# A two-layer diffusion trunk on one core: modulation products 512 columns wide, loaded from GpSimd's queue, and the state-space table products issued in whole runs

## The chip, the cores and the metric

The kernel runs on one core of one Trainium2 chip. The metric is the device time of one execution in microseconds (us). The time before is the median of three runs, 1136.7 us (1134.99 to 1141.31). The engines are named as the profile names them: PE (TensorE matmul), PEld (its weight loads), DVE (VectorE), ACT (ScalarE), POOL (GpSimd) and SP (SyncE, which only issues transfers here).

## The reference: what is computed

Two layers, in float32, on 128 context tokens and 256 latent tokens of width 1024. Only what bears on the change stands here:

```python
def ada_mods(cvec, p):
    m = jax.nn.silu(cvec) @ p['ada_w'] + p['ada_b']      # (1024) @ (1024 x 6144)
    return jnp.split(m[:, None, :], 6, axis=-1)          # shift, scale, gate, twice

def trunk_layer(x, cvec, p, mixer_fn):
    sh1, sc1, g1, sh2, sc2, g2 = ada_mods(cvec, p)
    mixed, extra = mixer_fn(rmsnorm(x, p['norm1_g']) * (1 + sc1) + sh1)
    x = x + g1 * mixed
    x = x + g2 * conv_ffn(rmsnorm(x, p['norm2_g']) * (1 + sc2) + sh2, p)
    return x, extra
```

The mixer has four parallel parts: neighbourhood attention, a bidirectional complex-diagonal state-space scan (S5), grouped-query attention and latent attention. The kernel does the scan in chunks of 8 tokens. For that it makes chunk tables from the S5 parameters alone, for each layer and each block of four channel groups: `SE` (inputs to chunk states), `SF` (states to outputs) and `SK` (the products inside a chunk). They are written to DRAM and loaded again in the scan.

## The kernel before, in words

**The main work.** All large products are `mm3` (L299 to L302): three float32r matmuls per 128 x 128 weight block, with weights and activations each split into a high and a low part. 1440 such triples make 4320 matmuls of 128 x 128 x up to 386 columns. Weight pieces of 512 KB come over SP's queue into three buffers with the tag `raw` (`piece`, L278), and ACT and DVE split them (`split1`).

**Modulation.** The vectors `silu(c) @ ada_w` for both token kinds are made a third of a layer at a time by `ada_steps(l, g)` (L317). The first third of layer 0 is made elsewhere (`first`), so five thirds are left. For each of the eight 128-row blocks `kc`, the weights come as two pieces `h` of 128 x 1024 in buffers of their own (tag `ada`, three buffers, `NADA`). The stationary operand is `cw[:, kc]`, 128 x 32 (two useful columns). Four matmuls per piece write 256 columns each to four different 32-partition strips of one PSUM bank `pa`: 16 pieces and 64 matmuls per third, 80 pieces and 320 matmuls in all. A piece is one step of the generator. Steps stand as the letter `A` in the string `SPEC`, which sets the order in which the mixer's streams advance; more are taken in the feed-forward part. The results are needed late, so these steps fill gaps between other work.

**Tables.** `s5_tables(l, ...)` (L693) runs over four blocks `b`. DVE makes `eb` and `ca` by complex multiplication (`cmul`), PE transposes eight 128 x 128 blocks of `eb` (L712), and PE makes the products `kd` (L728): 16 matmuls of 64 rows, 32 output partitions and 128 columns, over directions `d` (upper or lower 64 rows, two PSUM buffers), real and imaginary part `i` (accumulated) and group `g` (the 32-partition strip). Layer 0's tables are made beside the first mixer's projections. Layer 1's are made in layer 0's feed-forward part, at a lowered priority (L1334 to L1341).

**What sets the order.** The framework's scheduler orders each engine's instructions by priority and by when it takes operands to be ready. Each engine then runs its own list strictly in order, and waits on semaphores. The same holds for a queue of transfers: SP and POOL each issue in the order of their list, and a transfer into a reused buffer waits there for the buffer's readers. The helper `adjacent(calls)` (L247) issues the last call first and lets the others follow directly, so that the list holds them side by side. It is already used for the sums of squares and for the two heads in step.

**What else uses POOL's queue.** Stores of `SE`, `SF`, `SK` (L714, L721, L738), their loads in the scan (L749, L823), outputs, small clears, and one addition of the mask to the attention bias per pair of heads (L1168), which waits for the bias to be loaded over SP.

Of the kernel before, what the change touches and what calls it, by code (L numbers as in the profile page):

```python
# [20 lines left out]
L = 2  # L21
# [107 lines left out]
def _prepare(a):  # L129
    f = np.float32  # L130
    a = {n: np.asarray(v) for n, v in a.items()}
# [5 lines left out]
    def col(v, p=128):  # L137
# [7 lines left out]
    r["ada"] = np.stack([w.reshape(8, 128, 4, 2, 256).transpose(0, 3, 1, 2, 4)  # L145
                         for l in range(L) for w in np.split(a["ada_w"][l], 3, axis=1)][1:]
                        ).reshape(5, 8, 2, 128, 1024)
# [69 lines left out]
def _program(tc, I, O):  # L217
# [60 lines left out]
    def piece(src, n, tag="raw", eng=SY):  # L278
        raw = wp.tile([128, 1024], F32, name="raw", tag=tag, bufs=NRAW if tag == "raw" else NADA)
        eng.dma_start(raw[:, :n], src)  # L280
        return raw
# [35 lines left out]
    def ada_steps(l, g):  # L317
        acc = pa()
        for kc in range(8):
            for h in range(2):  # L320
                raw = piece(I["ada"][3 * l + g - 1, kc, h], 1024, "ada")
                for c in range(4):
                    PE.matmul(acc[32 * c:32 * c + 32, 256 * h:256 * h + 256], cw[:, kc],  # L323
                              raw[:, 256 * c:256 * c + 256], start=kc == 0 and h == 0,
                              stop=kc == 7 and h == 1)
                if kc < 7 or h == 0:
                    yield
        ar = kp.tile([128, 512], F32, name="ar", tag="sqz", bufs=3)
# [363 lines left out]
    def s5_tables(l, qp, cmp, bc, dd):  # L692
# [8 lines left out]
        for b in range(4):  # L701
# [6 lines left out]
            for i in range(2):  # L708
                e = kp.tile([128, 512], F32, name="tbo", tag="sqz", bufs=3)
                tr = pt()  # L710
                for g in range(4):
                    PE.transpose(tr[:, 128 * g:128 * g + 128], eb[:, i, g].rearrange("p j c -> p (j c)"), ident)  # L712
                A.activation(e, tr, AF.Copy)
                G.dma_start(SE[l][:, b, 512 * i:512 * i + 512], e)  # L714
# [9 lines left out]
            for d in range(2):  # L724
                h = slice(64 * d, 64 * d + 64)
                for i in range(2):
                    for g in range(4):
                        PE.matmul(kd[d][32 * g:32 * g + 32, 0:128], bb[i][h, 4 * b + g],  # L728
                                  ca[h, i, g, 2 * d:2 * d + 8].rearrange("p t c -> p (t c)"), start=i == 0,
                                  stop=i == 1)  # L730
# [865 lines left out]
```

## Time and profile before

| | us |
|---|---|
| median of the three runs | 1136.7 |
| the profiled execution, its own time | 1145.2 |
| its span, first to last instruction | 1143.2 |
| PE busy / DVE busy / ACT busy / POOL busy | 1074.7 / 798.3 / 581.0 / 86.8 |
| mean granted TensorE clock | 0.97 |

In a row of the timeline, the first number is the start in us from the span's start, the second the time from the first start to the last end; `x16` counts records. A float32 matmul leaves two records on PE, a float32r matmul and a transposition one. Matmuls are pipelined, so that what one costs is read from the start of one to the start of the next. In the lists of waits and the costliest groups, the engine's idle time stands with what ended it. The page's own span is 2 us shorter than the time of that execution.

### The profile page before, as it was taken

How to read it: one execution, taken by the hardware profiler on the slowest of the kernel's cores; microseconds unless marked ns; L12 is line 12 of the kernel's file. 1: busy time of each engine (PE TensorE's matmuls, PEld its weight loads, DVE VectorE, ACT ScalarE, POOL GpSimd, SP SyncE). 2: the span in 40 equal slices, each digit the busy share in tenths (PEclk: the TensorE clock that was granted, in tenths of full speed). 3: DMA queues.
4: the chain of work that ended last, by engine and by line, in shares of the span. 5: the costliest groups of instructions: out<-in, count | busy, mean ns of one | idle time of the engine just before them, and what ended most of it. 6: DMA issues, size and time to landing. Idle time of an engine off the chain costs nothing.

```text
span 1143.2 us, 18675 instructions
## 1 busy us (share of the span) xinstructions
PE 1074.7 (94%) x6724; PEld 911.6 (80%) x6724; DVE 798.3 (70%) x1934; ACT 581.0 (51%) x1251; POOL 86.8 (8%) x197
## 2 busy tenths in 40 slices
PE   6899889979999999999999989899799999999998
PEld 3677475437979999996999877545498999999998
DVE  6888478836979964676976886557468875467653
ACT  3654436426676543454456735563468554345532
POOL 4113111000100000000110220000000000000000
PEclk8899889979999999999999999999899999999999
DMA  9988847453465434443455664436133433443343
GB/s 342 298 274 270 264 128 270 139 178 129 147 196 161 138 100 138 147 117 113 136 153 159 180 222 159 111 124 230 39 111 99 135 113 114 137 138 117 117 133 100
DMA packets 64699, 182.18 MB, mean 159 GB/s; under 512 B 15840, under 2 KB 19168, under 8 KB 64608
## 3 DMA queue, kind: packets, MB, share of 16 engines
q1 hardware_dynamic: 55456, 152.52, 42.5%
q0 software_dynamic: 8576, 28.16, 7.8%
q8 instruction: 53, 0.87, 0.3%
q10 hardware_dynamic: 576, 0.32, 0.1%
q14 instruction: 38, 0.31, 0.1%
HBM read 166.19 MB, written 14.78 MB: 158 GB/s over the span
## 4 chain that ended last, share of the span: by engine, by line
PE 77%; DVE 9%; DMA 7%; ACT 4%; issue 1%; POOL 1%; SPq 0%; ACTq 0%; DVEq 0%; POOLq 0%
PE pz L300 12%; PE pz L301 11%; PE pz L302 11%; PE psc L300 8%; PE psc L301 8%; PE psc L302 8%; DMA raw<-ada 5%; PE pa L323 3%; PE psc L958 2%; PE ptr L971 2%; DVE lo L293 1%; PE po L996 1%; PE ptr L728 1%; DMA bias<-rpb 1%; PE psc L783 1%
## 5 line engine op out<-in xcount | busy, mean ns | idle before, releaser
L292 ACT ACTIVATE hi<-raw 128x512 fp32r<-128x512 f32 (+2 forms) x396 | 228.5, 585 | 285.6 <-PE pz L301 111.8
L293 DVE TENSOR_TENSOR lo<-raw,hi 128x512 fp32r<-128x512 f32 (+2 forms) x396 | 252.8, 640 | 158.5 <-ACT hi L292 114.4
L300 PE MATMUL pz<-ah,hi 128*128 128x386 f32 (+1 forms) x616 | 216.3, 353 | 3.7 <-ACT ah L430 2.2
L301 PE MATMUL pz<-al,hi 128*128 128x386 f32 (+1 forms) x616 | 213.7, 347 | 0.9 <-DVE al L431 0.8
L302 PE MATMUL pz<-ah,lo 128*128 128x386 f32 (+1 forms) x616 | 212.8, 346 | 0.0
L300 PEld LDWEIGHTS pz<-ah,hi 128*128 128x128 f32 x616 | 117.3, 191 | 23.5 <-issue 17.6
L301 PEld LDWEIGHTS pz<-al,hi 128*128 128x128 f32 x616 | 118.1, 192 | 7.0 <-issue 3.4
L302 PEld LDWEIGHTS pz<-ah,lo 128*128 128x128 f32 x616 | 117.9, 191 | 5.0 <-issue 4.4
L300 PE MATMUL psc<-ah,hi 128*128 128x386 f32 (+1 forms) x336 | 115.5, 344 | 0.3 <-DVE zr L461 0.3
L301 PE MATMUL psc<-al,hi 128*128 128x386 f32 (+1 forms) x336 | 115.4, 343 | 0.0
L302 PE MATMUL psc<-ah,lo 128*128 128x386 f32 (+1 forms) x336 | 115.0, 342 | 0.0
L323 PE MATMUL pa<-raw,cw 128*32 128x256 f32 x640 | 61.1, 418 | 18.7 <-DMA raw<-ada 18.6
L300 PEld LDWEIGHTS psc<-ah,hi 128*128 128x128 f32 x336 | 64.2, 191 | 1.6 <-issue 0.8
L301 PEld LDWEIGHTS psc<-al,hi 128*128 128x128 f32 x336 | 64.4, 192 | 0.4 <-issue 0.4
L302 PEld LDWEIGHTS psc<-ah,lo 128*128 128x128 f32 x336 | 64.3, 191 | 0.3 <-issue 0.2
L300 PE MATMUL pz<-fh,hi 128*128 128x384 f32 x176 | 59.7, 340 | 0.0
L300 PE MATMUL psc<-fh,hi 128*128 128x384 f32 x176 | 59.5, 338 | 0.0
L302 PE MATMUL psc<-fh,lo 128*128 128x384 f32 x176 | 59.5, 338 | 0.0
L302 PE MATMUL pz<-fh,lo 128*128 128x384 f32 x176 | 59.4, 337 | 0.0
L301 PE MATMUL psc<-fl,hi 128*128 128x384 f32 x176 | 59.1, 336 | 0.0
L301 PE MATMUL pz<-fl,hi 128*128 128x384 f32 x176 | 59.0, 336 | 0.0
L323 PEld LDWEIGHTS pa<-raw,cw 128*32 128x32 f32 x640 | 18.6, 114 | 45.2 <-DMA raw<-ada 25.5
(425 smaller groups left out, 1948.2 us busy)
## 6 DMA issues: line engine op xcount, KB each, us to landing
raw<-wup SPq DMA_DIRECT2D x88, 512.0 KB, 3.6
raw<-ada SPq DMA_DIRECT2D x80, 512.0 KB, 5.0
raw<-win SPq DMA_DIRECT2D x30, 512.0 KB, 5.1
raw<-wdn SPq DMA_DIRECT2D x32, 384.0 KB, 3.1
raw<-wdn SPq DMA_DIRECT2D x32, 320.0 KB, 2.9
a<-ada SPq DMA_DIRECT2D x16, 512.0 KB, 5.8
raw<-wout SPq DMA_DIRECT2D x16, 512.0 KB, 3.7
se<-tbo POOLq DMA_DIRECT2D x16, 256.0 KB, 4.2
```

The costliest lines, as they stand in the source:

```text
L292: A.activation(hi[:, :n], raw[:, a:b], AF.Copy)
L293: V.tensor_tensor(lo[:, :n], raw[:, a:b], hi[:, :n].bitcast(F32), op=OP.subtract)
L300: PE.matmul(out, wh, xh, start=start, stop=False)
L301: PE.matmul(out, wh, xl, start=False, stop=False)
L302: PE.matmul(out, wl, xh, start=False, stop=stop)
L323: PE.matmul(acc[32 * c:32 * c + 32, 256 * h:256 * h + 256], cw[:, kc], raw[:, 256 * c:256 * c + 256], start=kc == 0 and h == 0, stop=kc == ...
L728: PE.matmul(kd[d][32 * g:32 * g + 32, 0:128], bb[i][h, 4 * b + g], ca[h, i, g, 2 * d:2 * d + 8].rearrange("p t c -> p (t c)"), start=i == ...
L783: PE.matmul(e[:, NC * q:NC * q + NC], E[:, 128 * q:128 * q + 128], U[:, 4 * b + g], start=True, stop=True)
L958: adjacent([lambda j=j: PE.matmul(pair[:, j, :w], heads[j][0](b), heads[j][1](*keys), start=True, stop=True) for j in range(2)])
L971: PE.transpose(tr[:, 128 * kb:128 * kb + 128], P[:, 128 * kb:128 * kb + 128], ident)
L996: calls.append(lambda kb=kb, j=j: PE.matmul(o[64 * j:64 * j + 64, 128:T], heads[j][2](1 + kb), P3[j][:, kb].rearrange("p q c -> p (q c)"), ...
```

## The change

Three things change.

1. `ada_steps`: the weights are packed so that a piece holds two blocks of 512 columns instead of four of 256. A row block `kc` loads both of its pieces and then has four matmuls of 512 columns, issued side by side. The pieces are asked for on POOL's queue (`G`) instead of SP's. There are still 80 pieces and three buffers. The generator still has 16 steps a third: the first of a pair only asks for a piece, the second asks for the other and has the matmuls.
2. `s5_tables`: the four transpositions of one `eb` half are issued side by side.
3. `s5_tables`: the 16 products of a block are issued side by side, the imaginary part first.

```diff
-    r["ada"] = np.stack([w.reshape(8, 128, 4, 2, 256).transpose(0, 3, 1, 2, 4)
-                         for l in range(L) for w in np.split(a["ada_w"][l], 3, axis=1)][1:]
-                        ).reshape(5, 8, 2, 128, 1024)
+    r["ada"] = np.stack([w.reshape(8, 128, 2, 1024).transpose(0, 2, 1, 3)
+                         for l in range(L) for w in np.split(a["ada_w"][l], 3, axis=1)][1:])
...
         for kc in range(8):
+            raw = []
             for h in range(2):
-                raw = piece(I["ada"][3 * l + g - 1, kc, h], 1024, "ada")
-                for c in range(4):
-                    PE.matmul(acc[32 * c:32 * c + 32, 256 * h:256 * h + 256], cw[:, kc],
-                              raw[:, 256 * c:256 * c + 256], start=kc == 0 and h == 0,
-                              stop=kc == 7 and h == 1)
-                if kc < 7 or h == 0:
+                raw.append(piece(I["ada"][3 * l + g - 1, kc, h], 1024, "ada", G))
+                if h == 0:
                     yield
+            adjacent([lambda c=c: PE.matmul(acc[32 * c:32 * c + 32], cw[:, kc],
+                                            raw[c // 2][:, 512 * (c % 2):512 * (c % 2) + 512], start=kc == 0,
+                                            stop=kc == 7) for c in range(4)])
+            if kc < 7:
+                yield
...
-                for g in range(4):
-                    PE.transpose(tr[:, 128 * g:128 * g + 128], eb[:, i, g].rearrange("p j c -> p (j c)"), ident)
+                adjacent([lambda g=g: PE.transpose(tr[:, 128 * g:128 * g + 128],
+                                                   eb[:, i, g].rearrange("p j c -> p (j c)"), ident)
+                          for g in range(4)])
...
-            for d in range(2):
-                h = slice(64 * d, 64 * d + 64)
-                for i in range(2):
-                    for g in range(4):
-                        PE.matmul(kd[d][32 * g:32 * g + 32, 0:128], bb[i][h, 4 * b + g],
-                                  ca[h, i, g, 2 * d:2 * d + 8].rearrange("p t c -> p (t c)"), start=i == 0,
-                                  stop=i == 1)
+            calls = []
+            for i in (1, 0):
+                for g in range(4):
+                    for d in range(2):
+                        h = slice(64 * d, 64 * d + 64)
+                        calls.append(lambda i=i, g=g, d=d, h=h: PE.matmul(
+                            kd[d][32 * g:32 * g + 32, 0:128], bb[i][h, 4 * b + g],
+                            ca[h, i, g, 2 * d:2 * d + 8].rearrange("p t c -> p (t c)"), start=i == 1, stop=i == 0))
+            adjacent(calls[1:] + calls[:1])
```

Line numbers move a little: in the changed kernel `mm3` is L299 to L301, the modulation products are L324, the table products L731, `piece` is L279.

**PE, layer 0's feed-forward part, where layer 1's tables are made.** `bb` are the tables' stationary blocks, `ca` their moving ones, `pz` the feed-forward product. Before:

```order
L300 MATMUL pz<-ah,hi 128x386
L728 MATMUL ptr<-ca,bb_5098 32x128
L301 MATMUL pz<-al,hi 128x386
L728 MATMUL ptr<-ca,bb_5098 32x128
L302 MATMUL pz<-ah,lo 128x386
L728 MATMUL ptr<-ca,bb_5098 32x128
```

Changed:

```order
L299 MATMUL pz<-ah,hi 128x386
L731 MATMUL ptr<-ca,bb_5003 32x128 x8
L731 MATMUL ptr<-ca,bb_5002 32x128 x8
L300 MATMUL pz<-al,hi 128x386
```

Of layer 1's 64 table products, 24 stood alone between two large matmuls and 40 in five runs of 8; now all stand in four runs of 16. Layer 0's 64 stood in eight runs of 8 and now also stand in four runs of 16.

**PE, the end of layer 0's mixer, where modulation steps stand between attention heads.** `raw,cw` is a modulation product, `psc` the scores, `ptr` transpositions. Before:

```order
L323 MATMUL pa<-raw,cw 32x256 x9
L958 MATMUL psc<-gkT,gqT 128x384 x2
L971 MATMUL ptr<-cst,P 128x128 x3
L1280 MATMUL ptr<-cst,ty 96x128 x4
L323 MATMUL pa<-raw,cw 32x256 x4
L1280 MATMUL ptr<-cst,ty 96x128 x4
L971 MATMUL ptr<-cst,P 128x128 x3
L323 MATMUL pa<-raw,cw 32x256 x7
```

Changed:

```order
L324 MATMUL pa<-raw,cw 32x512 x4
L962 MATMUL psc<-gkT,gqT 128x384 x2
L975 MATMUL ptr<-cst,P 128x128 x3
L1284 MATMUL ptr<-cst,ty 96x128 x4
L324 MATMUL pa<-raw,cw 32x512 x4
L1284 MATMUL ptr<-cst,ty 96x128 x4
L975 MATMUL ptr<-cst,P 128x128 x3
L962 MATMUL psc<-mk,mq 128x128 x2
L324 MATMUL pa<-raw,cw 32x512 x4
```

Over the whole program the 320 modulation products stood in 62 runs of 1 to 12; now 160 stand in 40 runs of 4.

**POOL, the program's start and the first part of layer 0's mixer.** `s5bc` are S5 parameters, `sw`, `se`, `sf` table stores, `bias` the addition of the mask. Before, the start:

```order
L592 MEMSET PF_97 64x32
L645 DMA s5bc<-s5b 128x512
L646 DMA s5bc<-s5c 128x512
L648 DMA s5dd<-s5d 128x64
```

Changed, the start, and a later place:

```order
L593 MEMSET PF_97 64x32
L279 DMA raw<-ada 128x1024 x2
L646 DMA s5bc<-s5b 128x512
L647 DMA s5bc<-s5c 128x512
L649 DMA s5dd<-s5d 128x64
L279 DMA raw<-ada 128x1024
...
L279 DMA raw<-ada 128x1024 x2
L716 DMA se_105<-tbo 128x512
L1172 TENSOR_TENSOR bias<-bias,cst 128x1024
L279 DMA raw<-ada 128x1024
L716 DMA se_105<-tbo 128x512
```

On SP the first three of these loads stood behind all of the start's loads; now they stand near the head of POOL's list. Later ones stand among table stores, table loads and the bias addition.

## Rows read from the trace of the kernel before

**Rows 1.** The page: engines (busy us, share, instructions).

```profile
PE 1074.7 (94%) x6724; PEld 911.6 (80%) x6724; DVE 798.3 (70%) x1934; ACT 581.0 (51%) x1251; POOL 86.8 (8%) x197
```

**Rows 2.** The page's costliest groups, and the waits of SP's queue.

```profile
L323 PE MATMUL pa<-raw,cw 128*32 128x256 f32 x640 | 61.1, 418 | 18.7 <-DMA raw<-ada 18.6
SPq L280 <- PE pa L323: 165.8, 58, 13.8
```

**Rows 3.** Windows: us, busy us of PE, PEld, DVE, ACT, POOL; clock; DMA.

```profile
205.00:286.00 81.00, 70.85 (x496) 40.23 (x493) 47.50 (x139) 37.48 (x102) 0.71 (x4) 0.92 0.46 152
340.00:560.00 220.00, 220.00 (x1255) 207.92 (x1254) 159.20 (x307) 105.58 (x197) 5.19 (x9) 1.00 0.43 133
```

**Rows 4.** Timeline of PE, layer 0's feed-forward part, single table products.

```profile
522.77 0.40 PE L728 MATMUL ptr<-ca,bb 64*32 64x128 f32 x2
523.10 0.44 PE L301 MATMUL pz<-al,hi 128*128 128x386 f32 x1
523.48 0.40 PE L728 MATMUL ptr<-ca,bb 64*32 64x128 f32 x2
```

**Rows 5.** Timeline of PE, the same part, a run of 8 table products.

```profile
546.88 0.34 PE L301 MATMUL psc<-al,hi 128*128 128x386 f32 x1
547.06 0.34 PE L302 MATMUL psc<-ah,lo 128*128 128x386 f32 x1
547.33 0.45 PE L728 MATMUL ptr<-ca,bb 64*32 64x128 f32 x16
547.71 0.45 PE L300 MATMUL psc<-ah,hi 128*128 128x386 f32 x1
548.00 0.34 PE L301 MATMUL psc<-al,hi 128*128 128x386 f32 x1
```

**Rows 6.** Timeline of PE, mixers, modulation runs of one piece and of three.

```profile
686.86 0.33 PE L302 MATMUL pz<-ah,lo 128*128 128x384 f32 x1
687.12 0.64 PE L323 MATMUL pa<-raw,cw 128*32 128x256 f32 x8
687.69 0.44 PE L300 MATMUL pz<-ah,hi 128*128 128x384 f32 x1
687.97 0.34 PE L301 MATMUL pz<-al,hi 128*128 128x384 f32 x1
...
96.08 1.50 PE L323 MATMUL pa<-raw,cw 128*32 128x256 f32 x24
97.51 0.44 PE L300 MATMUL pz<-ah,hi 128*128 128x384 f32 x1
```

**Rows 7.** DMA issues in 57:130, 774:801 and 200:207: KB each, median us to landing.

```profile
raw<-ada SPq DMA_DIRECT2D x17, 512.0 KB, 6.7
...
raw<-ada SPq DMA_DIRECT2D x13, 512.0 KB, 4.3
...
tbef<-sf POOLq DMA_DIRECT2D x1, 512.0 KB, 3.9
```

**Rows 8.** Timeline of PE, end of layer 0's mixer, between two modulation runs (half clock).

```profile
237.66 1.65 PE L958 MATMUL psc<-gkT,gqT 64*128 64x384 f32 x4
239.25 0.90 PE L971 MATMUL ptr<-cst,P 128*128 128x128 f32 x3
239.94 1.06 PE L1280 MATMUL ptr<-cst,ty 128*96 128x128 f32 x4
240.93 1.08 PE L323 MATMUL pa<-raw,cw 128*32 128x256 f32 x8
```

**Rows 9.** Timeline of POOL, layer 0's mixer: the bias addition.

```profile
85.66 2.92 POOL L1168 TENSOR_TENSOR bias<-bias,cst 128x1024 f32<-128x1024 f32 x1 [2.76 <-DMA bias<-rpb]
```

**Rows 10.** The start: timeline of POOL and PE, and the window 5:10.

```profile
1.44 0.68 POOL L645 DMA_DIRECT2D s5bc<-s5b  x1
...
8.99 0.85 PE L396 MATMUL po<-sq,cst 128*32 128x384 f32 x8 [1.27 <-DMA cst<-cst]
...
5.00:10.00 5.00, 3.57 (x14) 1.38 (x12) 3.61 (x19) 1.32 (x4) 0.00 (x0) 1.00 1.05 397
```

## Prediction

> **What bounds the kernel now.** I read the page's engines first: PE is busy 1074.7 of 1143.2 us, the next engine, DVE, 798.3 [rows 1]. So what PE doesn't execute, and what it doesn't wait for, is what counts. Next, the windows tell apart two kinds of stretch [rows 3]. In layer 0's feed-forward part (340:560) PE is busy all 220.00 us at full clock: every microsecond taken off PE there comes off the end. At the end of layer 0's mixer (205:286) PE is busy 70.85 of 81 us, 87%, at a mean clock of 0.92: there a saved microsecond may turn into a wait. Then the costliest groups [rows 2]: the modulation products are busy 61.1 us, and PE is idle another 18.7 us just ahead of them, 18.6 of it for their loads. SP's queue stands 165.8 us waiting for PE to release a modulation buffer (same rows), and weight pieces queue behind it. PE is not late for weights in the feed-forward window all the same, so I charge nothing for freeing SP's queue; its worth is bounded by what PE idles at all, below.
>
> **A. Layer 1's tables, in the saturated stretch.** A single product and one large matmul repeat every 523.48 − 522.77 = 0.71 us [rows 4]; a large matmul alone takes 547.06 − 546.88 = 0.18 [rows 5], or 220.00 / 1255 = 0.175 over the window [rows 3], which I take. So a single product costs 0.53. With a run of 8 in between, the starts of two large ones stand 548.00 − 547.06 = 0.94 apart, two large steps of 0.35 in it: the run costs 0.59 [rows 5]. Most of either is the change from one kind of matmul to the other and back, not the columns. The modulation rows give that change apart: from its first product to the next large one a run of one piece takes 687.69 − 687.12 = 0.57, a run of three 97.51 − 96.08 = 1.43, so that a piece (four strips of 256 columns) is (1.43 − 0.57) / 2 = 0.43; and 687.97 − 686.86 = 1.11 less two large steps and that piece leaves 0.33 for the change of kind [rows 6]. The second half of a run of 16 adds products of 128 columns, by my estimate half a piece, 0.21 (0 if the two row halves run beside each other): 0.59 + 0.21 = 0.80. Before: 24 × 0.53 + 5 × 0.59 = 15.7. After: 4 × 0.80 = 3.2. **−12.5 us**, all on PE, all in the 100% stretch. The runs wait for `ca` as a whole, where singles took it as it came; DVE makes it, and is 159.20 of 220 us busy there [rows 3], so it is in time (0; it would show as PE idle in that window).
>
> **B. Layer 0's tables**, at the start: 8 × 0.59 before, 4 × 0.80 after, **−1.5 us**. The transpositions of `eb` fall from 25 runs to 15; I count 0, since no row shows what a change to a transposition costs; were it 0.33 each as for products, −3.3.
>
> **C. Modulation products on PE.** Four products of 256 columns cost 0.43, so four of 512 should cost 0.86. Before, the order has 62 runs, and 97 groups of up to four strips (a run that breaks a piece up has its strips in more groups): 62 × 0.33 + 97 × 0.43 = 62.2, beside 61.1 busy in the trace [rows 2]. After: 40 runs, 80 groups' worth of columns: 40 × 0.33 + 80 × 0.43 = 47.6. That is −14.6 at most. The mixers are 87% PE-busy [rows 3], and of a saving there I keep that share: **−12.7 us**. Bounds: −14.6, and 0 where all of it becomes waiting (D).
>
> **D. Waits for modulation loads.** Buffers: three, as before, but now a step needs two pieces at once. The second piece of a step goes into a buffer that the step before has read. Before, a piece's buffer was free three pieces, so one and a half of the new steps, ahead. Now a step can't follow the last one sooner than a load lands. A load of 512 KB lands 6.7 us after its issue at the start of the mixer and 4.3 in layer 1's, on SP; a load of that size from POOL's queue took 3.9 in a quiet place [rows 7]. I priced what stands between the 40 runs of the changed order with the steps of the trace: of the 39 intervals, 17 are shorter than 4.2 us, the four shortest at the end of layer 0's mixer some 2 us. The places are the head steps of [rows 8], where 237.66 to 240.93 are 3.3 us at half clock. What the short intervals lack adds up to 22.5 us with a landing of 4.2, 38.4 with 5.0, 49.9 with 5.5, 62.6 with 6.0, 82.1 with 6.7; with 6.7 in the first eight intervals, 5.0 in the next nine and 4.2 after, 35.8. Against the 18.6 now [rows 2] that is 17.2 more. I charge two thirds, **+11.5 us**: PE idles 1143.2 − 1074.7 = 68.5 us in all, most of it for other reasons, and where one of these comes next it swallows a step's delay. Bounds: 0, and all of the 82.1 (the rivals). While PE stands at a modulation product everything behind it on PE waits, since its list is in order. Heads in step then come later, and ACT and DVE with them, but these have slack. On POOL, a load can stand behind the bias addition, which takes 2.92 and waits 2.76 for its own load [rows 9], 5.7 together. I charge 0 here, because the next heads need that same bias; the slower rival takes it up. POOL issues 80 loads more, at 0.68 each [rows 10] some 54 us, beside 86.8 us busy in 1143: not a bound. SP issues 80 fewer.
>
> **E. The start.** Three loads, 1.57 MB, now stand near the head of POOL's list. In the window 5:10 the transfers are full, 397 GB/s at a share of 1.05, and PE's first product at 8.99 waited 1.27 for constants [rows 10]. The bytes ahead of x and the constants cost 1.57 MB at 397 GB/s, 3.9 us, if they come first, and 0 if they come behind: I take **+2.5**. The Trainium skill ("DMA: Bandwidth & Descriptors", section "Issuing engines are not separate DMA queues") says that transfers started by SP, ACT and GpSimd run on the same 16 engines and interleave. By it the whole 3.9 would be paid, and the sum below be −11.3; the full window agrees with it, but no run here shows these loads in that place.
>
> **The sum.** −12.5 − 1.5 − 12.7 + 11.5 + 2.5 = **−12.7 us**. The profiled execution took 1145.2, so the same one would take 1132.5. It was 8.5 us over the median of the three, 1136.7; I put the difference on the median: **1124.0 us**. The clock is not charged: its mean is 0.92 where PE idles most and 1.00 where it doesn't [rows 3], and the change takes some waits away and adds others; my ±3 us for it go into the range.
>
> **The rivals.** (1) *The waits don't grow*: loads are asked for a whole step earlier than PE comes to them, and no longer behind weights on SP. For it: SP's queue waits 165.8 us in all [rows 2], so part of today's 18.6 may be queueing. Against it: the buffer is released by PE's own last step. Then C counts in full and D is 0: −12.5 − 1.5 − 14.6 + 2.5 = −26.1, **1110.6 us**. (2) *Loads from POOL's queue come late*, at the place of [rows 8] and in layer 1's mixer alike. POOL's list is in order, and table stores, scan loads and bias additions stand among the loads, each waiting for another engine. If the loads land after 6.7 us everywhere, D is (82.1 − 18.6) × 2/3 = +42, and the sum −12.5 − 1.5 − 12.7 + 42 + 2.5 = +18: **1155 us**, slower than before. It decides from a mean landing of 6.0 us: there D is +29 and the sum +5. For it: the 6.7 at the mixer's start and the 5.7 of the bias addition; against it: the 3.9 from this very queue [rows 7]. The Trainium skill ("SBUF — State Buffer", section "SBUF: two separate sides") speaks for this rival and against the change: while DVE runs certain copies, GpSimd can't write the descriptors of its transfers, and it gives 3.1 us for one that takes 0.62 alone. No row here shows it. (3) *A tie*: loads land after 5.5 us on average, D is (49.9 − 18.6) × 2/3 = +20.9, and the sum −3.3: **1133.4 us**. It differs from the forecast in the landing alone, and DVE and POOL's list decide which. That the change doesn't do what it says is out: the changed order has the 40 runs of four and the table runs of 16.
>
> **How the numbers follow.** A measurement of this kernel can tell about 0.5%, 5.7 us, from no change: 1131.0 to 1142.4. I give the forecast 0.43, rival 1 0.17, the tie 0.23, rival 2 0.17. Faster is the forecast and rival 1, 0.60; within 0.5% 0.23; slower 0.17. The range takes in rival 1 with the clock's 3 us below it, 1107, the forecast, the tie, and up to a landing of 6 us with its sum of +5 and the clock's 3 above, 1145; the slower rival's own place is what is left out.
>
> **What would show it.** In the changed profile the table products of layer 1 stand in the feed-forward part as four groups of 32 records, each some 0.8 us between the large ones; PE has no idle time there. The modulation products' busy time is about 48 us, and PE's idle time ahead of them about 36, for the loads `raw<-ada`; under 20 would speak for rival 1, over 60 for rival 2. Loads from POOL's queue land after 4 to 5 us in the median. PE's first product stands at about 11.5 instead of 8.99. I am wrong in A if the run of 16 costs more than 2 us, or if PE stands idle there for `ca`; in C if four products of 512 columns take much over 0.86; and the whole forecast falls if PE's idle time in the mixers grows by more than its busy time shrinks.

## The result, and the profile after

The changed kernel takes **1151.6 us** (median of 4 runs, 1149.17 to 1154.36), the kernel before, run beside it, 1139.0 (4 runs): ratio **1.011**, 95% interval 1.006 to 1.016. It is slower; 1124.0 was forecast, with a range of 1107 to 1145. The profiled execution has a span of 1152.4 us against 1143.2, so 9.2 us are to be found (12.6 between the medians; both profiled executions are longer than the medians, that of before by 6 us, that of changed by 3). The page of the changed kernel, in order: engines, the modulation products with the idle time before them, the issue of their loads on POOL, and the loads with KB and median us from issue to landing.

```profile
PE 1059.5 (92%) x6404; PEld 900.4 (78%) x6404; DVE 792.7 (69%) x1934; ACT 582.2 (51%) x1251; POOL 127.9 (11%) x277
...
L324 PE MATMUL pa<-raw,cw 128*32 128x512 f32 x320 | 50.1, 703 | 37.1 <-DMA raw<-ada 37.1
L279 POOL DMA_DIRECT2D raw<-ada x80 | 42.8, 538 | 208.7 <-PE pa L324 204.2
...
raw<-ada POOLq DMA_DIRECT2D x80, 512.0 KB, 4.6
```

Against [rows 1, 2]: PE is busy 15.2 us less, as the change wants, and idle 92.9 us instead of 68.5, that is 24.4 more; −15.2 + 24.4 = 9.2. Of the idle time 37.1 stands ahead of the modulation products (18.7 before). The wait of SP's queue for PE's modulation reads is gone and stands on POOL now, 204.2.

Counted along the 4320 matmuls of the triples, which both kernels have, the 600th (late in layer 0's mixer) starts at 333.5 us instead of 316.6, the stretch from there to the 2100th takes 281.9 instead of 292.8, the next to the 2700th (layer 1's mixer) 242.5 instead of 239.5, and the rest 294.5 instead of 294.3. So layer 0's feed-forward part gains 10.9 us, and the start and the two mixers lose 19.9, most of it in layer 0.

Two windows of the kernel before, and then the windows of the changed kernel (columns as in [rows 3]; the clock is the number after the engines):

```profile
57.00:110.00 53.00, 49.71 (x455) 38.59 (x454) 46.92 (x72) 26.08 (x56) 13.56 (x17) 0.99 0.86 287
150.00:205.00 55.00, 49.69 (x325) 31.77 (x322) 43.87 (x107) 25.98 (x65) 10.60 (x15) 0.91 0.60 206
```

```profile
57.00:110.00 53.00, 43.19 (x343) 34.55 (x341) 41.23 (x69) 23.34 (x49) 14.13 (x21) 0.87 0.71 222
...
150.00:205.00 55.00, 41.49 (x263) 25.95 (x261) 33.34 (x85) 19.08 (x47) 13.65 (x22) 0.75 0.70 211
205.00:286.00 81.00, 70.71 (x440) 37.62 (x437) 51.71 (x149) 40.14 (x102) 14.67 (x28) 0.98 0.53 179
340.00:560.00 220.00, 217.40 (x1279) 211.84 (x1279) 169.42 (x343) 115.74 (x220) 7.10 (x15) 0.98 0.46 143
```

Most of the harm is in 57:110 and 150:205: PE is idle 9.8 and 13.5 us instead of 3.3 and 5.3, and the mean clock is 0.87 and 0.75 instead of 0.99 and 0.91. A mean clock counts the time at the lower of the two levels, 1.2 instead of 2.4 GHz: the whole program has 0.953 now and had 0.970, so PE stood at half clock for 2 × (1 − 0.953) × 1152.4 = 108 us instead of 69. The trace has PE busy in 84 us of that (64 before) and idle in 25 (4 before). In a stretch at half clock large products stand 0.32 us apart (26.78 to 27.10 at the start), at full clock 0.175. Taking half of the busy time there as lost, an estimate, 42 us go to the clock instead of 32. PE's busy time hides two things, then: some 25 us less work at full clock, and some 10 us given back because more of the rest ran at half speed (−25 + 10 = −15).

Layer 1's tables in the feed-forward part, timeline of PE in the changed kernel (columns as in [rows 4]):

```profile
552.58 0.34 PE L301 MATMUL psc<-ah,lo 128*128 128x386 f32 x1
552.85 0.67 PE L731 MATMUL ptr<-ca,bb 64*32 64x128 f32 x32
553.45 0.44 PE L299 MATMUL psc<-ah,hi 128*128 128x386 f32 x1
553.73 0.34 PE L300 MATMUL psc<-al,hi 128*128 128x386 f32 x1
```

A run of 16 costs 553.73 − 552.58 − 0.35 = 0.80, as forecast. From the 1680th to the 1920th of the 4320 matmuls of the triples the trace takes 49.66 us and took 60.53: −10.9. In 340:560 PE is idle 2.6 us now, 2.0 of it for ACT's `ah` and none for `ca`.

One of three long waits, in layer 0's mixer. First the DMA issues of 145:160 (KB each, median us to landing), then the timelines of SP's queue and of POOL, then two windows, all of the changed kernel:

```profile
raw<-ada POOLq DMA_DIRECT2D x4, 512.0 KB, 10.0
...
bias<-rpb SPq DMA_DIRECT2D x4, 128.0 KB, 13.2
raw<-wout SPq DMA_DIRECT2D x1, 512.0 KB, 14.4
```

```profile
148.07 5.12 SPq L1168 DMA_DIRECT2D bias<-rpb  x4
...
146.68 0.53 POOL L279 DMA_DIRECT2D raw<-ada  x1 [4.25 <-PE pa L324]
...
153.12 1.08 POOL L279 DMA_DIRECT2D raw<-ada  x2 [4.10 <-PE pa L324]
166.63 2.35 POOL L1172 TENSOR_TENSOR bias<-bias,cst 128x1024 f32<-128x1024 f32 x1 [12.44 <-DMA bias<-rpb]
```

```profile
158.00:166.20 8.20, 0.00 (x0) 0.00 (x0) 1.57 (x3) 0.00 (x0) 0.00 (x0) 0.62 0.73 214
166.20:198.00 31.80, 26.61 (x146) 15.50 (x148) 21.41 (x55) 14.58 (x36) 11.51 (x18) 0.71 0.69 222
```

The four bias loads, gathered in 256 B pieces, stand in flight when the second piece of the step is asked for at 153.12, after PE has read the step before. It lands at 166.2, and PE does nothing for the 8.2 us up to then. For the 31.8 us after it the mean clock is 0.71. The same happens at 64.6 to 72.7 and at 731.4 to 738.3, again with four bias loads in flight; the three waits are 23.4 of the 37.1 us, and the ten others 13.7. The Trainium skill ("DMA: Bandwidth & Descriptors", section "Issuing engines are not separate DMA queues") says that transfers of different issuing engines interleave on the same 16 engines; the rows agree, 10.0 us for a load from GpSimd beside bias loads from SyncE, 4.6 in the median.

The start, the first large product after and before:

```profile
26.29 0.69 PE L299 MATMUL pz<-ah,hi 128*128 128x384 f32 x1
```

```profile
23.70 0.69 PE L300 MATMUL pz<-ah,hi 128*128 128x384 f32 x1
```

### The profile page after: what moved, and what is told of

It is laid out like the page before. It is cut to its first block, busy times and chain, and to the rows that moved or that the text cites. A ratio compares the mean times of both kernels' runs of the same rounds, so it can differ in the third digit from the quotient of the medians.

```text
span 1152.4 us, 18052 instructions
## 1 busy us (share of the span) xinstructions
PE 1059.5 (92%) x6404; PEld 900.4 (78%) x6404; DVE 792.7 (69%) x1934; ACT 582.2 (51%) x1251; POOL 127.9 (11%) x277
## 4 chain that ended last, share of the span: by engine, by line
PE 62%; issue 15%; DVE 9%; DMA 8%; POOL 3%; ACT 3%; SPq 0%; POOLq 0%; DVEq 0%; ACTq 0%
PE pz L299 10%; PE pz L300 10%; PE pz L301 10%; PE psc L299 8%; PE psc L300 8%; PE psc L301 8%; DMA raw<-ada 4%; PE pa L324 2%; DVE lo L292 2%; POOL raw L279 1%; DMA bias<-rpb 1%; DMA a<-ada 1%; DMA tbw<-sw 1%; PE psc L787 1%; PE po L1000 1%
## 5 line engine op out<-in xcount | busy, mean ns | idle before, releaser
L299 PE MATMUL pz<-ah,hi 128*128 128x386 f32 (+1 forms) x616 | 215.1, 352 | 4.5 <-ACT ah L431 2.8
L301 PE MATMUL pz<-ah,lo 128*128 128x386 f32 (+1 forms) x616 | 211.3, 344 | 0.0
L299 PEld LDWEIGHTS pz<-ah,hi 128*128 128x128 f32 x616 | 118.0, 192 | 24.5 <-issue 15.8
L301 PEld LDWEIGHTS pz<-ah,lo 128*128 128x128 f32 x616 | 118.9, 193 | 1.8 <-issue 1.7
L299 PE MATMUL psc<-ah,hi 128*128 128x386 f32 (+1 forms) x336 | 114.7, 341 | 0.3 <-DVE zr L462 0.3
L301 PE MATMUL psc<-ah,lo 128*128 128x386 f32 (+1 forms) x336 | 114.5, 341 | 0.0
L324 PE MATMUL pa<-raw,cw 128*32 128x512 f32 x320 | 50.1, 703 | 37.1 <-DMA raw<-ada 37.1
L279 POOL DMA_DIRECT2D raw<-ada x80 | 42.8, 538 | 208.7 <-PE pa L324 204.2
L299 PEld LDWEIGHTS psc<-ah,hi 128*128 128x128 f32 x336 | 63.8, 190 | 1.1 <-DVE zr L462 0.6
L301 PEld LDWEIGHTS psc<-ah,lo 128*128 128x128 f32 x336 | 64.0, 190 | 0.0
L301 PE MATMUL pz<-fh,lo 128*128 128x384 f32 x176 | 59.6, 339 | 0.0
L299 PE MATMUL pz<-fh,hi 128*128 128x384 f32 x176 | 59.5, 338 | 0.1
L299 PE MATMUL psc<-fh,hi 128*128 128x384 f32 x176 | 59.4, 338 | 0.0
L301 PE MATMUL psc<-fh,lo 128*128 128x384 f32 x176 | 59.4, 337 | 0.0
```

Of the source, the lines that this page charges most:

```text
L299: PE.matmul(out, wh, xh, start=start, stop=False)
L301: PE.matmul(out, wl, xh, start=False, stop=stop)
L324: adjacent([lambda c=c: PE.matmul(acc[32 * c:32 * c + 32], cw[:, kc], raw[c // 2][:, 512 * (c % 2):512 * (c % 2) + 512], start=kc == 0, st ...
```

## The experiments

Every run was timed beside executions of before, whose median wandered from 1139 to 1146, so ratios to that before are compared; 0.1% is 1.1 us. "Half clock" is 2 × (1 − mean clock) × span of the profiled execution; "loads" is PE's idle time for modulation loads, "other idle" the rest of span minus PE's busy time. These three columns are of one execution each.

| run | median us | ratio, 95% | loads | other idle | half clock |
|---|---|---|---|---|---|
| before | 1139.0 | 1 | 18.6 | 49.9 | 69 |
| changed | 1151.6 | 1.011 (1.006 to 1.016) | 37.1 | 55.8 | 108 |
| e1 tables only | 1126.2 | 0.986 (0.983 to 0.989) | 15.1 | 52.7 | 59 |
| e2 changed, loads on SyncE | 1135.9 | 0.995 (0.992 to 0.998) | 14.2 | 68.2 | 66 |
| e3 before, loads on GpSimd | 1144.7 | 1.003 (1.000 to 1.005) | 19.6 | 49.9 | 64 |
| e4 changed, no loads | 1120.1 | 0.982 (0.978 to 0.986) | 0 | 70.8 | 81 |
| e5 tables only, no loads | 1113.2 | 0.975 (0.971 to 0.979) | 0 | 62.0 | 62 |
| e6 tables only, 1/8 of the products | 1127.0 | 0.987 (0.981 to 0.992) | 0 | 95.2 | 120 |
| e7 changed, even bias | 1129.2 | 0.988 (0.983 to 0.992) | 21.0 | 55.9 | 81 |
| e8 changed, bias on GpSimd | 1145.6 | 1.004 (1.000 to 1.007) | 22.7 | 74.5 | 90 |
| e9 tables only, loads on GpSimd | 1135.3 | 0.993 (0.989 to 0.996) | 20.2 | 56.1 | 59 |
| e10 tables only, even bias | 1112.1 | 0.972 (0.968 to 0.977) | 8.7 | 46.7 | 44 |
| e11 changed, smaller buffers | 1146.5 | 1.003 (1.000 to 1.007) | 39.2 | 52.0 | 96 |
| e12 e11 and four buffers | 1136.4 | 0.995 (0.992 to 0.998) | 17.3 | 63.0 | 82 |
| e13 e2 and extra products | 1126.5 | 0.986 (0.980 to 0.992) | 16.4 | 53.7 | 38 |
| e14 changed and extra products | 1142.8 | 0.999 (0.997 to 1.002) | 33.7 | 50.0 | 59 |
| e15 tables only, packed bias | 1112.3 | 0.976 (0.969 to 0.983) | 9.6 | 47.6 | 47 |

Over all executions the half clock of before is 41 to 90 us (median 64), of changed 92 to 108, e1 51 to 63, e2 63 to 89, e4 74 to 81, e5 44 to 62, e6 108 to 120, e11 70 to 103 (median 89), e12 75 to 91 (81), e13 38 to 61 and e14 57 to 69. Over 70 executions of before, in which nothing differs but the run, the time rises by some 0.35 us for each us of half clock (correlation 0.87). That says what goes together, not which comes first: a late load makes both.

No run changes only what its diff says, since the framework's scheduler makes the order of each engine anew. Of the 6084 PE records that aren't modulation products, some 240 stand in another order in e13 than in e2, some 320 in e6 than in e5, some 120 in e4 than in e5, and some 200 in e11 than in changed. e11 only takes buffers away, and it is still 5 us (medians) to 9 us (ratios) faster than changed. So a single difference of under 1% can be one of order. (e15 and e10 have the same order, and the same median to 0.2 us.) Outside the start and the two mixers all kernels with whole table runs agree within 2 us (281.0 to 282.9 from the 600th to the 2100th matmul, 294.2 to 295.5 from the 2700th on).

**The parts: queue and width.** e1 is the kernel before with the second and third part of the change and no other edit.

> The kernel before with the table parts of the change alone (transpositions and products in whole runs), modulation untouched. Theory (the loss lies in the modulation steps: two pieces wanted at once, half of them asked for only when the last step has read, and PE's clock falls in the waits): 12 to 14 us faster than before, about 1126, idle time for modulation loads 15 to 22 as before, half clock for about 70 us. Rival (the long table runs themselves hold up PE in layer 0's mixer, where they wait for whole tables): 0 to 5 us faster, and layer 0's mixer ends later than before.

0.986, some 16 us less: the table parts are good for all that was forecast of them (14.0) and a little more. In the profiled executions 10.9 of 18.0 us stand between the 1680th and the 1920th matmul, and 7.7 ahead of the 600th, where B's 1.5 were expected; where the rest of those comes from wasn't traced. e2 is the changed kernel with

```diff
-                raw.append(piece(I["ada"][3 * l + g - 1, kc, h], 1024, "ada", G))
+                raw.append(piece(I["ada"][3 * l + g - 1, kc, h], 1024, "ada"))
```

> The changed kernel with the modulation pieces back on SyncE's queue, all else as changed. Theory (two pieces at once, three buffers): about as slow as the changed kernel, 1146 to 1156, PE idle for modulation loads 28 to 40. Rival (GpSimd's queue is at fault: its ordered list and its slower transfers): waits fall to 20 or less, 1115 to 1128.

The waits are as the rival had them, 14.2; the time is neither's. It is 1.6% faster than the changed kernel, but 0.9% (10 us) slower than e1, which wide products were to beat. Its page, engines and modulation products:

```profile
PE 1047.6 (93%) x6404; PEld 896.3 (79%) x6404; DVE 793.8 (70%) x1934; ACT 581.3 (51%) x1251; POOL 86.0 (8%) x197
...
L324 PE MATMUL pa<-raw,cw 128*32 128x512 f32 x320 | 46.2, 653 | 14.3 <-DMA raw<-ada 14.2
```

e1's:

```profile
PE 1057.4 (94%) x6724; PEld 906.6 (81%) x6724; DVE 797.3 (71%) x1934; ACT 581.1 (52%) x1251; POOL 86.7 (8%) x197
...
L323 PE MATMUL pa<-raw,cw 128*32 128x256 f32 x640 | 61.2, 411 | 15.3 <-DMA raw<-ada 15.1
```

The products are 15.0 us shorter, as forecast (14.6), and PE's busy time falls by 9.8. (By the estimate above that is some 12.4 us less work at full clock, and 2.6 given back.) But PE's idle time for things other than these loads rises from 52.7 to 68.2. So the theory with which the experiments began (waits for paired loads) fell as the sole cause. e3 is the kernel before with `G` in its `piece` call, and e9 the same edit in e1.

> The kernel before with the modulation pieces asked for on GpSimd's queue, products still 256 columns wide and a step still one piece. Theory: the queue alone does little, 1134 to 1144, waits for modulation loads 15 to 25. Rival (GpSimd's queue is at fault): waits of 30 or more, 1148 to 1160.

> The tables-only kernel with the modulation pieces on GpSimd's queue, products still 256 columns and one piece a step: with the tables-only run, the wide one on SyncE's queue and the changed kernel it makes a square of queue by width. Theory (it takes both: a step that wants two pieces and a queue on which the bias loads go ahead): 1126 to 1133, waits for modulation loads 15 to 25. Rival (GpSimd's queue costs the same 16 us at either width): 1138 to 1146.

e3 answers as the theory has it, 1.003 with 19.6 of waits (its median is 0.6 us over the range, and the before beside it 3.8 us over that of the result). e9 is between its two expectations, 1135.3 where the theory went to 1133 and the rival began at 1138: 0.65% (7 us) slower than e1. The square: widening costs 0.9% on SyncE's queue and 1.8% on GpSimd's; the queue costs 0.65% with narrow steps and 1.6% with wide ones. So width harms alone; the queue does so in e9, while the same edit cost 0.3% (0.0 to 0.5) in e3. What belongs to both together is some 0.9%, 10 us by the ratios and 6.6 by the medians; by the four intervals it is anything from 0.2 to 1.7%.

**No loads.** Three pieces are loaded once and read by every step, in the changed kernel (e4) and in e1 (e5):

```diff
+    held = []
+    def held_piece(src, n, tag, eng=SY):
+        if len(held) < NADA:
+            held.append(piece(src, n, tag, eng))
+            return held[-1]
+        held.append(held[len(held) % NADA])
+        return held[-1]
...
-                raw.append(piece(I["ada"][3 * l + g - 1, kc, h], 1024, "ada", G))
+                raw.append(held_piece(I["ada"][3 * l + g - 1, kc, h], 1024, "ada", G))
```

> The changed kernel with only the first three modulation pieces loaded and read again by all steps (the other 77 loads are left out), so that nothing of a modulation step waits. Theory: the 37 us of idle time ahead of these products go, and with them most of the added half-clock time (110 down to 50 to 75 us): 1095 to 1110. If the half clock comes from something else (the denser products, the longer runs), it stays near 110 us and the time near 1115 to 1120.

> The kernel of the tables-only run, products still 256 columns wide, with only the first three modulation pieces loaded (77 loads left out). It is to be compared with the changed kernel without loads, 1120.1. Theory now (in the mixers PE waits for the chains of ACT and DVE, the modulation products only fill its gaps, so that narrower products cost nothing by themselves): 1114 to 1125, PE's idle time for all other reasons some 10 us below the 70.8 of that run. Rival (the 14 us of PE time that wide products save are real and were lost in that run to the clock): at or above the tables-only run's 1126.

e4's time is what the rival had named for it, with only part of the half clock gone (108 to 81 us): the waits for loads are 37 us of idle time, but leaving them out bares 15 us of other waits. And e5, with the narrow products, is 0.7% *faster* than e4, although its products keep PE busy for 49.8 us and e4's for 40.3. The rows of e5, then of e4:

```profile
L332 PE MATMUL pa<-raw,cw 128*32 128x256 f32 x640 | 49.8, 396 | 1.2 <-DVE ar L338 1.2
```

```profile
L333 PE MATMUL pa<-raw,cw 128*32 128x512 f32 x320 | 40.3, 610 | 0.0
```

Without any wait for a load, the wide products still don't win. The rival in e5's expectation is out.

**Less and more work in the modulation steps.** e6 takes seven of eight row blocks out of e1:

```diff
-        for kc in range(8):
+        for kc in range(1):
...
+        for _ in range(14):
+            yield
```

> The kernel of the tables-only run with one of eight row blocks of each modulation third (7/8 of the modulation products and their loads left out), some 53 us of PE time and 15 us of waits less. Theory (filler): the time falls by 20 to 40, 1086 to 1106, and PE's other idle time in the mixers grows by 25 or more. Rival (PE bounds the mixers too): by 60 or more, 1066 or less.

Neither, and the filler theory's 20 us at least are missed too: it gains nothing at all on e1 (0.987 against 0.986), though PE has 53 us less of products and no wait for loads. Against e5, which also has next to no loads, it is 1.2% (14 us) slower, with 42 us of work less. The window 100:280 (the mixer) of e5, then of e6:

```profile
100.00:280.00 180.00, 168.25 (x1316) 110.16 (x1319) 126.52 (x367) 92.45 (x232) 20.91 (x36) 0.97 0.33 89
```

```profile
100.00:280.00 180.00, 146.24 (x861) 97.90 (x860) 117.44 (x333) 85.29 (x219) 20.21 (x35) 0.85 0.34 91
```

In the same time e6's PE executes 861 records instead of 1316. 384 of the 455 that are missing are the modulation products themselves, but of the others, too, it gets 785 done instead of 856. It is idle 33.8 us instead of 11.8, and has a mean clock of 0.85 instead of 0.97; DVE and ACT get less done too. What PE waits for in e6, and then for the softmax in e5, whole program:

```profile
PE psc L963 <- ACT P L945: 17.6, 9, 2.7
PE ptr L1448 <- ACT ar L1442: 10.0, 5, 4.6
PE psc L788 <- ACT P L938: 9.2, 2, 7.8
```

```profile
PE psc L970 <- ACT P L952: 5.3, 3, 2.5
PE psc L795 <- ACT P L945: 3.9, 1, 3.9
```

`P` is the softmax of a pair of heads: PE waits 26.8 us for it in these two groups with the products gone, and 9.2 with them. (The waits for `ar` stand at the start and are in e5 too, 11.3.) So the products had filled PE's waits. The other direction, in e2 (e13) and in the changed kernel (e14):

```diff
...
+            more = [lambda c=c, kc=kc: PE.matmul(acc[32 * c:32 * c + 32, 0:256], cw[:, kc],
+                                                 raw[c // 2][:, 512 * (c % 2):512 * (c % 2) + 256],
+                                                 start=False, stop=False) for c in range(4)]
+            adjacent(full[:3] + more + full[3:] if kc == 0 else more[:3] + full + more[3:])
```

> The wide kernel on SyncE's queue (1135.9, 0.995 of before) with four more products of 256 columns in every modulation step, on the same pieces and added to the same sums: 160 products and, at 0.43 us for four, 17 us of PE work more, about what the wide form had saved. Theory (the modulation products fill PE's gaps; work taken out of them comes back as idle time and half clock): the time does not rise, 1124 to 1140, PE's other idle time falls by 8 us or more. Rival (PE bounds the mixers): 17 us more, 1148 to 1157.

> The changed kernel with the same 17 us of extra products. Theory: within 6 us of the changed kernel either way, since the extra work stands in the steps that also wait for loads. Rival (PE bounds the mixers): 12 to 17 us slower than the changed kernel, 1163 or more.

(`full` are the step's own four products, as in the changed kernel.) With 160 useless products more, e13 is 0.9% and e14 1.2% *faster* than without them; e14 beats even what the theory had for it. e13's page, then e14's:

```profile
PE 1050.2 (94%) x6724; PEld 897.3 (80%) x6724; DVE 794.3 (71%) x1934; ACT 581.1 (52%) x1251; POOL 85.7 (8%) x197
```

```profile
PE 1056.5 (93%) x6724; PEld 901.5 (79%) x6724; DVE 792.0 (69%) x1934; ACT 581.2 (51%) x1251; POOL 127.7 (11%) x277
```

PE is only 2.6 us more busy than in e2, with 17 us (40 × 0.43) more of work, since the half clock falls from 66 to 38 us; other idle time falls from 68.2 to 53.7. In e14 half clock falls from 108 to 59. The rival, a PE bound in the mixers, wanted 17 us more time and is out. At 0.35 us each, the 30 to 34 us less of half clock (medians) are worth 11 to 12 us, about what was gained; that the clock and not the new order did it is argued by this, not tested apart.

**The three long waits.** e7 reads the bias as whole rows of another tensor, e10 does the same in e1; e8 asks for the bias on GpSimd's queue.

```diff
-                    SY.dma_start(bias[64 * (rq % 2):64 * (rq % 2) + 64, rq // 2].rearrange("p r h c -> p (r h) c"),
-                                 bass.AP(tensor=I["rpb"].tensor, offset=l * 1860 + c * 930 + (7 - rq) * 62 - 48,
-                                         ap=[[1, 64], [31, 8], [1, 64]]))
+                    SY.dma_start(bias[64 * (rq % 2):64 * (rq % 2) + 64, rq // 2].rearrange("p r h c -> p (r h c)"),
+                                 I["ada"][0, rq, c][0:64, 0:512])
```

> The changed kernel with the attention bias read as whole 2 KB rows of another tensor (same 128 KB a load, so the bias's values are left out) instead of 256 B pieces. Theory (the three waits of 7 to 8 us stand behind the bias loads, which go ahead on SyncE's queue now, and the half clock follows these waits): no wait for a modulation load over 4 us, their sum 20 or less, half clock 60 to 85 us instead of 110, 1126 to 1140. Rival (GpSimd's queue is late by itself): sum of waits 30 or more, 1146 to 1156.

> Control for the changed kernel with the even bias (which was 22 us faster than the changed one): the tables-only kernel with the same even bias. Theory (the uneven bias loads hurt through the waits of the paired steps on GpSimd's queue): it gains 8 us or less on the tables-only run, 1118 to 1126. Rival (the even bias helps every kernel alike): 1100 to 1110.

> The changed kernel with the bias loads asked for on GpSimd's queue too, so that they stand in one list with the modulation loads. Theory (order against the bias loads decides): the long waits go or move, 1128 to 1144. Rival (not the order; GpSimd's queue has too much in it): as slow as the changed kernel or slower, 1148 to 1165.

PE's waits for modulation loads (us, times, longest), changed and then e7:

```profile
PE pa L324 <- DMA raw<-ada: 37.1, 13, 8.3
```

```profile
PE pa L324 <- DMA raw<-ada: 21.0, 12, 4.9
```

In e7 the long waits are gone (longest 4.9 instead of 8.3; sum 21.0; both a little over what was expected), half clock falls to 81, and the ratio from 1.011 to 0.988. The order on PE is nearly that of the changed kernel (some 40 records moved). But e10 gains 1.4% on e1 as well, more than the theory allowed and less than the rival: the uneven bias loads hold up any version, and the changed kernel only some 10 us more. e8 gains 0.75% on the changed kernel: its waits for modulation loads are 22.7, but other waits are 74.5, among them 8.3 for a softmax and 7.7 for the scan. It tells little.

e12 has a fourth modulation buffer; to make room, `NAH` goes from 9 to 8 and the tag `sq` from 5 to 4 buffers, which e11 does alone.

> Control for the next run: the changed kernel with eight instead of nine pairs of split activations and four instead of five row buffers, which makes room for a fourth modulation buffer that this one does not have. All theories: near the changed kernel, 1146 to 1160; what it differs by is the price of the smaller buffers.

> The changed kernel with four modulation buffers (and the smaller other buffers of the run before), so that both pieces of a step are asked for when the step before the last has read. Theory (the second piece comes late because its buffer comes free late): against the run before, waits for modulation loads fall from 30 to 40 to 15 or less, half clock falls by 20 us or more, the time by 12 to 25 us. Rival (loads from GpSimd's queue are late whenever they are asked for, or other engines take up what is gained): within 6 us of the run before.

The fourth buffer takes the waits for loads from 39.2 to 17.3 and the half clock from 96 to 82. The rows of the modulation products, e11 and then e12:

```profile
L324 PE MATMUL pa<-raw,cw 128*32 128x512 f32 x320 | 48.9, 687 | 39.2 <-DMA raw<-ada 39.2
```

```profile
L324 PE MATMUL pa<-raw,cw 128*32 128x512 f32 x320 | 46.2, 654 | 17.7 <-DMA raw<-ada 17.3 <-DVE ar L330 0.4
```

The time falls by 0.85%, 10 us, short of the 12 that were expected at least: of 21.9 us of waits for loads, 11 come back as other idle time (52.0 to 63.0). That these 10 us are also about what queue and width cost together beyond each alone may be chance.

**The version that the runs point to.** e15 is e1 with the bias rows laid out in DRAM as the loads want them (the same values, copied out of the table when the inputs are packed), so that each of the 64 partitions reads 2 KB in one piece.

> The tables-only kernel with the attention bias packed in DRAM as the rows that a load wants (its values kept), 2 KB rows instead of 256 B pieces: the version that the runs point to. Expected: as the tables-only run with even bias, 1104 to 1116. Rival (that run was fast because of its false bias values): 1122 to 1130.

0.976 (0.969 to 0.983): faster than before by 2.4%, and than the changed kernel. It keeps the bias's values, so it isn't its false ones that make e10 fast. The bias loads of e1, and then of e15 (KB each, median us to landing):

```profile
bias<-rpb SPq DMA_DIRECT2D x16, 128.0 KB, 8.9
```

```profile
bias<-rpq SPq DMA_DIRECT2D x16, 128.0 KB, 4.3
```

The packed rows differ from the table in three things: the length of a piece, where it starts (the table's pieces start one element further from partition to partition), and that the table's pieces overlap. Which of these costs the time isn't shown.

## Why the prediction was wrong

**A, tables in the feed-forward part: right.** 0.80 for a run of 16, and 10.9 of the 12.5 us in the stretch. **B** (−1.5) lies inside e1's 16 us and was not measured alone. Step by step, the forecast had −14.0 for A and B, −12.7 for C, and 14.0 for D and E. The runs had −16 for the tables (e1), +10 for wide products on SyncE's queue (e2), and +16 to +18 for GpSimd's queue on top.

**C failed, and it is the step that made the forecast wrong.** "Of a saving there I keep that share", 87%, −12.7. The saving on PE was there: 50.1 us busy against 61.1 (about 48 forecast), and 46.2 in e2, where PE is less at half clock. But PE's busy share of a stretch doesn't say that PE sets its end. The mixers, as far as the waits show, go at the pace of the heads' and the scan's chains through ACT and DVE; modulation steps stand in the gaps of those. Taking 15 us out (e1 to e2) gave 15.5 us more of other idle time and cost 10 us in time; taking some 10 out without any loads (e5 to e4) cost 7; taking some 42 out (e5 to e6) cost 14; putting 17 in gained 10 (e2 to e13) and 9 to 14 (changed to e14). The size of any one of these may hold a good part of new order. That 42 us of work less bring nothing is beyond that, and all five have one sign. The right term for C was 0, or somewhat above.

**The clock**, "not charged" but for ±3 in the range, is the likely reason why the sign is against it. Idle time of PE comes with half clock: in e6 the mixer's clock goes from 0.97 to 0.85 when the filler goes. In the changed kernel half clock rose from 69 to 108 us. PE was idle in half of the added time, and in the other half it lost some 10 us. In the accounts of the two profiled executions that is the largest term missing: work at full clock fell by 25.2 (28.6 worked out on PE), the clock took 10.0 (0), waits for loads rose by 18.5 (11.5) and other idle time by 5.9.

**D: the number was close, and that was luck.** The waits rose from 18.6 to 37.1, by 18.5; 17.2 more had been worked out, and I charged two thirds of it, for idle time elsewhere that would swallow the rest. Other idle time rose instead, 49.9 to 55.8. The 17.2 were spread over 17 short intervals, for steps that want two pieces from three buffers. But on SyncE's queue the steps want the same, and the waits are 14.2 (e2). What the changed kernel has more are three places where the load meets the bias loads and takes 10 to 13 us. The buffers are half of that: a second piece is asked for only when the step before has read, and with a fourth buffer (e12) the waits are 17.3 instead of 39.2 and the time 10 us less (e11). In the trace of before three of the ten loads that are in flight beside bias loads also take 10.5 to 12.9 us, the others 5.1 to 7.4. Narrow steps need one piece and not two, which may be why they ride over that (e9 has one such wait, of 8.2 us).

**E: right.** The first large product comes 2.6 us later, 2.5 were taken. With wide loads on SyncE's queue it stands at 23.75 (e2), with narrow ones on GpSimd's at 25.83 (e3), so it is the queue that moves it. The statistics' first product, which I had named as the mark, did not come later (8.72); it was the large product behind it.

**The rivals.** The slower one gave 1155, close to the time, but for loads that all land late; the median landing is 4.6, not 6. Its closeness is luck. The Trainium skill's rule beside it ("SBUF — State Buffer", section "SBUF: two separate sides": GpSimd can't write descriptors while DVE runs certain copies) would slow those that meet such a copy; the median of 4.6 from GpSimd's queue, beside 5.0 from SyncE's in the kernel before and 4.4 in e2, shows no such delay for most of them, and no run tests it for single ones. Rival 1, free of waits, is e2 or e4 in effect: 26 us faster was worked out for it, 5 and 21 were measured, for want of C above all.

**The signs.** Two that were to speak for the forecast came out, 50.1 us of modulation products (48) and 37.1 of idle time ahead of them (36), and the time didn't: neither of them asks whether a saving reaches the end. The last sign did, and came true against the forecast: PE's idle time grew by 24.4 us and its busy time shrank by 15.2.

**Open:** which chain takes up the time saved in e2 was not followed further than the list of waits (softmax, scan); how much of each difference under 1% is the scheduler's new order has no test (none keeps the order and changes the work alone); and the 7 us that GpSimd's queue costs with narrow steps (e9), 2 of them at the start, have no test of their own.

## What to carry to other kernels

A saved microsecond counts where the engine is busy all of the time; where it is at 87% and waits for several short chains (the end of layer 0's mixer here), ask first what else would end earlier. If work fills gaps, try to leave it out altogether (e6): if the time stays, making it cheaper is worth nothing, and may cost clock. Where a scheduler makes the order anew, run one version that changes nothing of use (e11), to see what a new order alone can do. When a step comes to need two buffers at once, give it a whole step's buffers ahead, and look for what is in flight where its second load is asked for.

## What was not expected of the hardware

Useless matmuls made the program faster: 160 products more, and 0.9 to 1.2% less time, with the half clock down from 66 to 38 and from 108 to 59 us. And bias loads gathered in 256 B pieces out of a small table are costly beyond their size: four loads of 128 KB per pair of heads, two pairs a layer, cost 12 to 16 us of 1126 (e10, e15), as against the same bytes in 2 KB rows.
